# Moving the early ada_w loads to GpSimd's queue and setting the compression's tail one step apart

## The chip, the core and the metric

The kernel runs on one core of one Trainium2 chip. The core has five engines that work beside each other, each in the order of its own queue: TensorE (PE; its weight loads are PEld), VectorE (DVE), ScalarE (ACT), GpSimd (POOL) and SyncE (SP), which here only asks for transfers. A transfer is asked for by an engine's queue and carried out by 16 DMA engines. The metric is the device time of one execution in microseconds, the median of several runs.

## What is computed

One block of a network in float32: 512 tokens of width 2048. Six vectors of 2048 come from one condition row `c`; the first norm, a mixer of convolutions and attention, a residual, the second norm and a gated feed-forward follow. Cut to what the change touches:

```python
sh_a, sc_a, g_a, sh_f, sc_f, g_f = jnp.split(jax.nn.silu(c) @ ada_w[l] + ada_b[l], 6, axis=-1)
h = modulate(rms_norm(x, norm_mix[l]), sh_a, sc_a)
proj = h @ w_in[l]
...
def compress(kv, pe, w1, b1, w2):
    ...
    blocks = kv[:, idx] + pe[None, None, :, None, :]
    hid = jax.nn.gelu(jnp.einsum('bnlgd,ldh->bngh', blocks, w1) + b1)
    return jnp.einsum('bngh,he->bnge', hid, w2)
...
k_cmp = compress(k_cmp_raw, pe_k, k_w1, k_b1, k_w2)
v_cmp = compress(v_cmp_raw, pe_v, v_w1, v_b1, v_w2)
k_cmp = apply_rope(rms_norm(k_cmp, k_norm[0]), cos[:, cmp_end], sin[:, cmp_end])
...
x = x + g_a[:, None, :] * (jnp.concatenate([y_conv, y_attn], axis=-1) @ w_out[l])
h = modulate(rms_norm(x, norm_ffn[l]), sh_f, sc_f)
x = x + g_f[:, None, :] * ((jax.nn.silu(h @ ffn_w1[l]) * (h @ ffn_w3[l])) @ ffn_w2[l])
```

`sh_f`, `sc_f` and `g_f`, which the second half needs, depend on `c` and `ada_w` alone, so they can be summed at any time before.

## The kernel before

Every large product is made of three products of parts: a weight tile is loaded (`raw`), rounded by ScalarE to a high part (`whi`, L92) and completed by VectorE with a low part (`wlo`, L93), and `mm3` (L96 to L100) multiplies the parts. Weight tiles pass through a ring of four `raw`, three `whi` and three `wlo` buffers. PSUM has four banks called `main` for long sums and four called `aux` for everything else.

The stretch around the change is the one between the first stage and the convolutions. Three pieces of work share it:

- `token_blocks` (L702): two blocks of columns of `w_in`, each over 16 chunks of the width, two chunks at a time, for four groups of 128 tokens. That makes 2 x 8 product steps of 24 products; after each the generator yields. The four sums of a block stand in the four `main` banks. `take_kv` and `take_q` read them (`normed_rope`, L514 to L532) and so free the banks, which the convolutions (`conv`, L895) need next.
- `before_attention` (L674): eight norm steps, then `compress` (L576). The compression multiplies blocks of `raw_kv` with its own weights in eight steps (L633), adds the bias into `hid` (L641), takes the Gelu (L642), and ends with a tail: transposes of `hid` (L648) copied to `hidT` (L650), the product `pk` (L653) with norm and rotation (`normed_rope`, which ends in `u` at L531), the transpose of `u` (L657), and the value products (L668) copied to `v4` (L671). Its small late weights and biases are already asked for by GpSimd (L622, L626).
- `early` (L715): the first three of the parts of `ada_w` that the second norm needs, `ffn_part` for j = 0, 1, 2. Each part is summed by `ada` (L173): 16 tiles of 128 x 512 are loaded one by one into a ring of two buffers (`wring`, L512) and added with a factor by VectorE (L187, L189); then four transposes and a reduction (`ada_cols`) write columns of `gsc` or `shf`.

`beside` (L440) lets the early parts take 3, later 2, at last 4.8 of their steps after each product step; `weave` (L102) lets `before_attention` take 1.5 steps after each. A step is the code from one `yield` to the next. This sets the order of the program text. The order in which each queue issues is set from it by a planner, which lets an instruction pass another that it expects to be late; each engine then works through its queue strictly in that order and waits on semaphores.

In the tail there are three yields between the Gelu and the transposes of `hid`, none between these and `pk`, one ahead of the transpose of `u`, and one at the end.

A second, later user of the same functions is `gates_beside` (L959): it sums further parts beside the convolutions, with the tiles of other tensors as places.

## Time and profile before

| | us |
|---|---|
| median of three runs | 2181.52 |
| lowest and highest | 2179.64, 2182.79 |
| span of the profiled execution (first to last instruction) | 2174.9 |
| granted TensorE clock, share of full speed | 0.998 |

The profile is of one execution. Its span is 6.6 us less than the median of the runs; what lies between is ahead of the first and behind the last instruction. A row of a timeline reads: start, length, engine, line, operation, what is written and read, and in brackets how long the engine idled just ahead and what ended that. A row of a waits view reads: who waited, for whom, microseconds in total, times, longest. A landing is the time from the issue of a transfer until its data are there. Product rows have a modelled length and overlap; two starts in a row tell the pace.

### The profile page before, as it was taken

The numbers are of one execution on the slowest core, as the hardware profiler recorded it, in microseconds if no ns is written. First come the engines' busy times: TensorE is split into PE (matmuls) and PEld (weight loads), VectorE is DVE, ScalarE is ACT, GpSimd is POOL, SyncE is SP. The second block draws the span as 40 slices with busy tenths as digits, with TensorE's granted clock in tenths as the row PEclk, the third lists the DMA queues.
The fourth block names the chain that finished last, engine by engine and source line by source line (L and its number), as shares of the span: only waits on it lengthen the run. The fifth ranks groups of instructions, "written<-read, shape, count | busy, mean of one in ns | idle before, by whom it ended". The sixth has DMA issues, their size and how long they took to land.

```text
span 2174.9 us, 31018 instructions
## 1 busy us (share of the span) xinstructions
PE 2143.3 (99%) x11513; PEld 1799.9 (83%) x11513; DVE 1722.8 (79%) x2574; ACT 1007.8 (46%) x1622; POOL 222.9 (10%) x273
## 2 busy tenths in 40 slices
PE   7999999999999999999999999999999999999999
PEld 5788768888888888888888888888888888888887
DVE  5978869977886665988787878888787887878788
ACT  5335334555555223744444444444444455444543
POOL 2410000000000100000000000000000112111210
PEclk9999999999999999999999999999999999999999
DMA  9965768754654985387777777677776499797976
GB/s 339 365 233 166 255 205 256 234 157 148 177 156 138 287 290 170 93 219 185 187 174 175 166 179 185 173 170 171 184 177 172 105 305 284 154 299 143 288 158 142
DMA packets 442315, 438.39 MB, mean 202 GB/s; under 512 B 18468, under 2 KB 349260, under 8 KB 441524
## 3 DMA queue, kind: packets, MB, share of 16 engines
q1 hardware_dynamic: 373184, 327.50, 48.1%
q0 software_dynamic: 68448, 108.44, 24.1%
q8 instruction: 90, 1.47, 0.3%
q14 instruction: 61, 0.50, 0.1%
q10 hardware_dynamic: 532, 0.48, 0.1%
HBM read 416.39 MB, written 19.96 MB: 201 GB/s over the span
## 4 chain that ended last, share of the span: by engine, by line
PE 89%; DVE 5%; DMA 4%; issue 1%; ACT 0%; SPq 0%; DVEq 0%; ACTq 0%
PE main L1209 15%; PE aux L1209 11%; PE aux L1567 9%; PE main L1567 9%; PE main L1211 8%; PE main L98 7%; PE main L99 7%; PE main L100 7%; PE aux L1211 6%; DMA araw<-in_ada_w 2%; PE aux L98 2%; PE aux L100 2%; PE aux L99 2%; DVE acc L189 2%; PE aux L860 1%
## 5 line engine op out<-in xcount | busy, mean ns | idle before, releaser
L1195 ACT CAST whi<-raw 128x1024 fp32r<-128x1024 f32 x246 | 258.0, 1049 | 285.6 <-PE main L1209 107.1
L1209 PE MATMUL main<-hC,whi 128*128 128x512 f32 x1408 | 353.5, 392 | 1.4 <-ACT whi L1195 1.4
L1195 ACT CAST whi<-t 128x1024 fp32r<-128x1024 f32 x186 | 195.4, 1051 | 263.7 <-PE aux L1209 70.3
L1202 DVE TENSOR_TENSOR wlo<-raw,whi 128x1024 fp32r<-128x1024 f32 x218 | 266.1, 1221 | 54.9 <-ACT whi L1195 49.9
L1209 PEld LDWEIGHTS main<-hC,whi 128*128 128x128 f32 x1408 | 253.3, 189 | 47.6 <-ACT whi L1195 1.6
L1209 PE MATMUL aux<-hC,whi 128*128 128x512 f32 x1072 | 268.9, 392 | 0.0
L1209 PEld LDWEIGHTS aux<-hC,whi 128*128 128x128 f32 x1072 | 192.9, 189 | 34.4
L1211 PEld LDWEIGHTS main<-hC,wlo 128*128 128x128 f32 x1408 | 192.0, 190 | 13.6
L1211 PE MATMUL main<-hC,wlo 128*128 128x256 f32 x1408 | 196.3, 282 | 0.0
L98 PE MATMUL main<-alo,whi 128*128 128x512 f32 x448 | 182.3, 407 | 3.6 <-DVE alo L372 2.7
L100 PE MATMUL main<-ahi,whi 128*128 128x512 f32 x448 | 176.4, 394 | 0.0
L99 PE MATMUL main<-ahi,wlo 128*128 128x512 f32 x448 | 176.3, 394 | 0.0
L92 ACT CAST whi<-raw 128x1024 fp32r<-128x1024 f32 (+2 forms) x84 | 79.6, 951 | 203.1 <-PE main L100 124.0
L1211 PEld LDWEIGHTS aux<-hC,wlo 128*128 128x128 f32 x1072 | 146.3, 190 | 10.4
L1211 PE MATMUL aux<-hC,wlo 128*128 128x256 f32 x1072 | 149.6, 282 | 0.0
L1539 DVE TENSOR_TENSOR wlo<-t,whi 128x1024 fp32r<-128x1024 f32 x102 | 124.2, 1220 | 29.1 <-ACT whi L1195 29.0
L1185 POOL DMA_DIRECT2D t<-in_ffn_w x42 | 65.0, 1547 | 794.8 <-DVE d L1216 656.3
L93 DVE TENSOR_TENSOR wlo<-raw,whi 128x1024 fp32r<-128x1024 f32 (+2 forms) x84 | 91.5, 1093 | 51.4 <-ACT whi L92 51.0
L1202 DVE TENSOR_TENSOR wlo<-t,whi 128x1024 fp32r<-128x1024 f32 x84 | 102.6, 1222 | 37.0 <-ACT whi L1195 37.0
L1216 DVE TENSOR_TENSOR d<-aux,d 128x256 f32<-128x256 f32 x168 | 70.9, 422 | 62.2 <-PE aux L1211 62.1
L1567 PE MATMUL aux<-whi,glo 128*128 128x512 f32 x308 | 119.8, 389 | 0.0
L1567 PE MATMUL aux<-whi,ghi 128*128 128x512 f32 x308 | 119.8, 389 | 0.0
(363 smaller groups left out, 4314.0 us busy)
## 6 DMA issues: line engine op xcount, KB each, us to landing
raw<-in_ffn_w SPq DMA_DIRECT2D x204, 512.0 KB, 5.1
t<-in_ffn_w POOLq DMA_DIRECT2D x90, 512.0 KB, 7.5
t<-in_ffn_w SPq DMA_DIRECT2D x78, 512.0 KB, 4.5
araw<-in_ada_w POOLq DMA_DIRECT2D x56, 512.0 KB, 14.4
kT<-in_ada_w SPq DMA_DIRECT2D x100, 256.0 KB, 3.9
raw<-in_w_in SPq DMA_DIRECT2D x128, 192.0 KB, 2.7
araw<-in_ada_w SPq DMA_DIRECT2D x40, 512.0 KB, 7.2
raw<-in_w_in SPq DMA_DIRECT2D x37, 512.0 KB, 9.3
```

The source lines that it names most:

```text
L92: nc.scalar.copy(hi[:, :m], raw[:, :m])
L93: nc.vector.tensor_sub(lo[:, :m], raw[:, :m], hi[:, :m].bitcast(F32))
L98: nc.tensor.matmul(ps, lhs[0], rhs[1], start=first, stop=False)
L99: nc.tensor.matmul(ps, lhs[1], rhs[0], start=False, stop=False)
L100: nc.tensor.matmul(ps, lhs[0], rhs[0], start=False, stop=last)
L1195: hi_ins[-1] = nc.scalar.copy(hi, t).ins
L1202: lo_ins[-1] = nc.vector.tensor_sub(lo, t, hi.bitcast(F32)).ins
L1209: nc.tensor.matmul(ps, wt[0][:, ks[k]], hc(p, k), start=first and k == 0, stop=False, skip_group_check=True)
L1211: nc.tensor.matmul(ps[:, HS:], wt[1][:, ks[k]], hc(p, k)[:, 0:HS], start=False, stop=last and k == HK - 1, skip_group_check=True)
L1216: nc.vector.tensor_add(to, ps[:, h * HS:(h + 1) * HS], to)
L1539: W["last"] = nc.vector.tensor_sub(lo, t, hi.bitcast(F32)).ins
L1567: nc.tensor.matmul(ps[2 * t + c], x_[:, j, tok], w[:, cs], start=m == 0 and j == 0 and p in (1, 5, 2), stop=m == 2 and j == GS[b] - 1 and ...
```

## The change

`ada`, `ffn_part` and `ffn_parts` get an argument `q`, the queue that asks for the `ada_w` tiles; it is SP's where nothing is said, and GpSimd's for `early`. The later users keep SP. In the compression's tail one yield moves from ahead of the transposes of `hid` to behind them, ahead of `pk`, and a second yield is added ahead of the transpose of `u`.

```diff
-    def ada(ring, width, c0, n, got, bias=False):
+    def ada(ring, width, c0, n, got, bias=False, q=nc.sync):
...
-            nc.sync.dma_start(rv, ada_v[:, k0:k0 + step, c0:c0 + n])
+            q.dma_start(rv, ada_v[:, k0:k0 + step, c0:c0 + n])
...
-    def ffn_part(ring_, width, j):
+    def ffn_part(ring_, width, j, q=nc.sync):
...
-            yield from ada(ring_, width, (3 + m) * D + j * 512, 512, got)
+            yield from ada(ring_, width, (3 + m) * D + j * 512, 512, got, q=q)
...
-            yield from ada(ring_, width, 5 * D + cs.start, 512, got, bias=True)
+            yield from ada(ring_, width, 5 * D + cs.start, 512, got, bias=True, q=q)
...
-    def ffn_parts(ring_, width, js):
+    def ffn_parts(ring_, width, js, q=nc.sync):
         for j in js:
-            yield from ffn_part(ring_, width, j)
+            yield from ffn_part(ring_, width, j, q)
...
         yield
         yield
-        yield
         for h in range(2):
             pt = aux()
             nc.tensor.transpose(pt[:, :P], hid[:, h * P:(h + 1) * P], ident)
             for m in range(2):
                 nc.vector.tensor_copy(hidT[:, m, h, :], pt[:, at_m[m]])
+        yield
         pk = aux()
         for h in range(2):
             nc.tensor.matmul(pk[:NP_, :HD], hidT[:, 0, h, :], cw2[0][h], start=h == 0, stop=h == 1)
         u = normed_rope(pk[:NP_, None, :HD], 1, "c", 0, NP_)
+        yield
         yield
         pt = aux()
...
-    early = ffn_parts(wring, 512, range(3))
+    early = ffn_parts(wring, 512, range(3), nc.gpsimd)
```

## The prediction

> **What bounds the kernel now.** First the head of the page.

> ```profile
> span 2174.9 us, 31018 instructions
> ...
> PE 2143.3 (99%) x11513; PEld 1799.9 (83%) x11513; DVE 1722.8 (79%) x2574; ACT 1007.8 (46%) x1622; POOL 222.9 (10%) x273
> ```

> TensorE is busy for 2143.3 of 2174.9 us, so an edit that removes none of its products can give back only waits of TensorE. The edits lie between the end of the first stage and the start of the convolutions, so the second view is who TensorE waited for between 187 and 330 us (total, times, longest).

> ```profile
> PE aux L657 <- DVE ru L531: 1.5, 1, 1.5
> PE aux L653 <- DVE hidT L650: 1.3, 1, 1.3
> PE main L98 <- DVE rq L522: 0.9, 1, 0.9
> PE main L98 <- DVE wlo L93: 0.8, 1, 0.8
> PE main L98 <- DVE rw L529: 0.8, 1, 0.8
> ```

> Five waits, 5.3 us together: this is the whole prize, 0.24% of the time. The first two, 2.8 us, are in the compression's tail. The window from 310 to 320 (PE, PEld, DVE, ACT and POOL busy, granted clock, DMA share, GB/s) has the end of the tail and the last of them.

> ```profile
> 310.00:320.00 10.00, 8.88 (x41) 6.98 (x42) 9.33 (x26) 5.87 (x25) 0.00 (x0) 1.00 0.66 185
> ```

> The clock is full, so nothing is throttled; TensorE has 1.1 us to spare, VectorE only 0.7. What stands behind the waits is told by the chain of waits from 282 to 322 us (start, length, what).

> ```profile
> 314.63 0.76 DVE acc L189
> 315.41 2.78 DMA araw<-in_ada_w
> 318.28 0.75 DVE acc L189
> 319.04 0.33 DVE rw L529
> ...
> 319.52 0.47 PE main L98
> ```

> The reader is to see a ring of two `araw` tiles: a sum (L189) ends, the next load is asked for 0.02 us later (314.63 + 0.76 = 315.39, issue at 315.41), and 2.8 us pass until the tile is there. TensorE's 319.52 product, the first of the convolutions, stands at the end of that ring. The sums' own view from 284 to 320 us gives their count, their length and what VectorE idled for ahead of them (us, times):

> ```profile
> L189 DVE SCALAR_TENSOR_TENSOR acc<-araw,cT,acc x16: 737/752/753, 284.2 to 318.3; 128x512 f32<-128x512 f32 x16
> ...
>   DMA araw<-in_ada_w: 8.7, 7
> ```

> Sixteen sums in 34.1 us are 2.1 us each, 4.3 for a round trip of the two tiles. So VectorE, which works in order, is held up by loads for the second norm, which comes after the attention, and TensorE sees it only where something that it needs stands behind.

> **The tail's steps.** TensorE's timeline, then VectorE's, around the tail, and the Gelu's row of ScalarE:

> ```profile
> 301.98 0.38 PE L648 MATMUL aux<-const,hid 128*128 128x128 f32 x2
> ...
> 302.43 0.40 PE L99 MATMUL main<-whi,alo 128*128 128x512 f32 x1
> 304.10 0.69 PE L653 MATMUL aux<-late,hidT 128*62 128x128 f32 x4 [1.28 <-DVE hidT L650]
> ...
> 308.05 0.39 PE L99 MATMUL main<-whi,alo 128*128 128x512 f32 x1
> 308.27 0.39 PE L100 MATMUL main<-whi,ahi 128*128 128x512 f32 x1
> 310.20 0.24 PE L657 MATMUL aux<-const,ru 62*128 62x62 f32 x1 [1.54 <-DVE ru L531]
> ```

> ```profile
> 293.06 0.87 DVE L641 TENSOR_TENSOR hid<-aux,late 62x256 f32<-62x256 f32 x2
> ...
> 298.48 1.54 DVE L189 SCALAR_TENSOR_TENSOR acc<-araw,cT,acc 128x512 f32<-128x512 f32 x2 [2.98 <-DMA araw<-in_ada_w]
> ...
> 303.83 0.60 DVE L650 COPY hidT<-aux 128x62 f32<-128x62 f32 x4
> ...
> 306.85 0.75 DVE L189 SCALAR_TENSOR_TENSOR acc<-araw,cT,acc 128x512 f32<-128x512 f32 x1 [2.16 <-DMA araw<-in_ada_w]
> ...
> 309.77 0.28 DVE L531 TENSOR_TENSOR ru<-ru,rq 62x128 f32<-62x128 f32 x1
> ...
> 313.41 1.19 DVE L671 COPY v<-aux 32x128 f32<-32x128 f32 x4
> ```

> ```profile
> 295.30 0.42 ACT L642 ACTIVATE hid<-hid 128x256 f32<-128x256 f32 x1
> ```

> A product step is 24 products of the kind of L99 and L100, 0.22 us apart (308.05 to 308.27): 5.3 us. The diff moves the two transposes of `hid` one step earlier and the transpose of `u` one step later, and keeps the product `pk` (L653). It adds no instruction. The moved last step also issues a memset on POOL (L661), which ran 70 us ahead of its use and stays free.

> Transposes of `hid`: they go from 302.0 to about 296.5. The Gelu ends at 295.72, so they can run. Their copies (L650, 0.60) fall into VectorE's idle 2.98 us ahead of 298.48, or right behind that pair of sums, at 300.6; both are ahead of 302.0. The wait of 1.28 goes: **-1.28**.

> Transpose of `u`: `pk` ends at 304.79, `u` (L531) at 310.05, 5.3 us later. One product step is 5.3 us, so with the same delays the wait of 1.54 just closes. Two sums stand in that stretch on VectorE, and each may come later from the other queue (below). I keep 0.5 of the wait: **-1.0**. The ends are -1.54 and 0.

> What follows in that step, the `v` products (L668) and copies, is behind L657 as before and reaches VectorE at nearly the same hour, since the waits ahead of it shrink as it moves back. Cost taken: 0. If it came a whole step later, its copies, twice the 1.19 us of L671, would stand with the first take of the convolutions' main banks, and the wait there would be up to 2.4 longer.

> **The queue.** Forty-eight triggers (three parts of 16 tiles) leave SP for POOL. On SP each takes 0.33 us and nobody waits for SP's time itself, so removing them alone gives 0. The raw tiles of `w_in` behind them would be asked for sooner, and the one wait on their split (0.8, L93) may shrink; no row tells whether its load was late by SP or by the ring's place. Between 0 and -0.8 I take 0.

> On POOL the descriptor work and the landing of loads of the same size (128 rows of 512 floats) show as follows; the first pair of rows is today's load on SP (187 to 330 us), then `k<-gd`, then `cc<-rsd`, each with its landing row (min, median, max), and last the `araw` loads of the first stage, twice as large.

> ```profile
> L183 SPq DMA_DIRECT2D araw<-in_ada_w x46: 327/334/545, 193.5 to 315.4; - x46
> DMA to landing us min/median/max: 2.8/3.7/6.9
> ```
> ```profile
> L1373 POOL DMA_DIRECT2D k<-gd x44: 539/547/595, 1728.6 to 2032.9; - x44
> DMA to landing us min/median/max: 3.0/7.5/12.8
> ```
> ```profile
> L935 POOL DMA_DIRECT2D cc<-rsd x8: 568/574/590, 370.9 to 704.0; - x8
> DMA to landing us min/median/max: 3.4/5.0/5.5
> ```
> ```profile
> L276 POOL DMA_DIRECT2D araw<-in_ada_w x56: 751/751/923, 28.0 to 124.0; - x56
> ```

> The `k` loads come in bursts, so their median holds their own queue; their least, 3.0, is a load alone, 0.2 over SP's least. `cc` reads one row for all partitions; its median is 1.3 over SP's. The trigger is slower as well:

> ```profile
> 106.49 1.54 DVE L291 SCALAR_TENSOR_TENSOR acc<-araw,cT,acc 128x512 f32<-128x512 f32 x2
> ```
> ```profile
> 108.36 0.75 POOL L276 DMA_DIRECT2D araw<-in_ada_w  x1 [1.19 <-DVE acc L291]
> ```

> The sums end at 108.03, POOL starts at 108.36: 0.33 against SP's 0.02. So one round trip of the ring costs 0.51 more (0.31 + 0.2) to 1.61 more (0.31 + 1.3). Below nothing: on SP an `araw` load lines up behind the raw tiles of `w_in`, and its longest landing is 6.9; with a queue of its own the least of 3.0 could come back, so a single round trip may also gain some 3.5. Of the two the lower is nearer, because `k` has the same shape and plain source, and the gain on crowded ones offsets part of it.

> From 293 (where VectorE turns to `hid`, L641) to the first convolution product at 319.5 are 26.5 us, six round trips of 4.3. If VectorE kept its order, that product would come 6 x 0.51 = 3.1 to 6 x 1.61 = 9.7 later. But the order is not the text's: L99 stands between L648 and L653, where the text has no step, so a planner sets it from expected readiness, and a slower ring puts fewer sums ahead of the take. In the last ten microseconds VectorE hardly idles at all (9.33 busy), so there its own work, sums among it, is the limit. Between 0 and the 3.1 to 9.7 I take **0** for the ring, its cover being VectorE's idle 8.7 us and the fact that nobody waits for the sums themselves.

> POOL has other work behind the new triggers:

> ```profile
> 239.19 0.31 POOL L661 MEMSET hrep<- 128x256 f32 x1 [94.51 <-PE aux L584]
> 274.81 0.57 POOL L622 DMA_DIRECT2D late<-in_cmp_k_b  x1 [35.31 <-DVE acc L189]
> ...
> 290.62 0.31 POOL L639 MEMSET hid<- 128x256 f32 x1 [12.56 <-PE aux L633]
> ```

> The memset of `hid` may stand behind a trigger that waits for a sum; VectorE adds at 293.06, over 2 us later, and triggers come some 2.1 us apart, like the sums, so 0, with 2 at the worst. Triggers may stand behind L622, which waited 35.31 us for its buffer; six loads of 0.57 are 3.4 us of POOL once, ahead of the 293 from which I count. I take 0.

> **The sum.** -1.28 - 1.0 + 0 = -2.3 us: span 2174.9 - 2.3 = 2172.6. The median of the runs, 2181.5, lies 6.6 over the profiled span (launch and end); with the same 6.6 the forecast is **2179.2**. A measurement here can tell about 0.2% (4.4 us) from no change, so this counts as no change.

> **Rivals.**
> 1. All goes: with fewer sums ahead of the take, the convolutions' start (0.9) and the split (0.8) go too: 1.28 + 1.54 + 0.9 + 0.8 = 4.5, 2177.0. For it: VectorE's 9.33 just there is partly sums. Against: it needs every wait to close. Chance 0.18.
> 2. A wait takes the place of those removed: the chain shows the ring, not the tail, ahead of 319.52. TensorE gets there 2.3 earlier and waits 2.3 longer for L529; or the planner puts the tail's pieces where they stood. 2181.5. Chance 0.18.
> 3. Slower: the ring at POOL's price with sums still ahead of L529. Place: VectorE's queue ahead of the first `q` take. It decides from the point where six round trips cost more than the tail gives back at the convolutions, and is beyond 4.4 from 0.73 a trip on. 3.1 to 9.7 dearer, 2184.6 to 2191.2, about 2187. For it: the median of `cc`. Against: planned order, and loads no longer behind raw tiles. Chance 0.22.

> [...]

> **How the numbers follow.** Forecast 0.42, rivals 0.18, 0.18 and 0.22. Faster by over 0.2% (under 2177.2): most of rival 1 and the forecast's edge, 0.18. Slower (over 2185.9): most of rival 3 and a little of 2, 0.20. Within: 0.62. The range goes from rival 1 with a margin, 2176.0, to the middle of rival 3, 2187.0.

> **What would show it.** Right: L653 and L657 gone from TensorE's waits, `hidT` copied a product step ahead of `pk`, loads from POOL landing in 3 to 4 us, first convolution product near 317. Wrong: that product at or after 319.5 behind sums that wait for `araw`; landings of 5 us and more; POOL's memset of `hid` after 293; or a shift past 330 us, where nothing was edited.

## The result, and the profile after

The kernel became slower: 2192.12 us against 2181.13 us (medians of five runs each, 2190.40 to 2195.49 and 2179.35 to 2182.79), a ratio of 1.0055 with a 95% interval from 1.0043 to 1.0067. That is 12 us by the ratio, or 11.0 by the medians. The prediction's range ended at 2187.0.

The head of the page after (span, and the busy line of section 1):

```profile
span 2190.3 us, 31035 instructions
PE 2151.1 (98%) x11513; PEld 1806.8 (82%) x11513; DVE 1722.9 (79%) x2574; ACT 1007.1 (46%) x1622; POOL 248.3 (11%) x321
```

TensorE runs the same 11513 products and is busy 7.8 us longer with them. POOL has 48 instructions more, the triggers, and 25.4 us more of busy time.

The two spans differ by 15.4 us, more than the medians, because the profiled execution before was a quick one (its span lies 6.6 us under the median, that of after 1.8) and because the stretch starts at another time in each. So the stretch itself is measured. (In every run listed the time lies 1.7 to 2.1 us over its span. So of the 6.6 us that the part on the time before, and the prediction's sum after it, put ahead of the first and behind the last instruction, some 4.8 are only that quick execution.) These are TensorE's timelines before and after, at the first product of the token blocks and at the first of their ninth step:

```profile
200.57 0.50 PE L98 MATMUL main<-wlo,ahi 128*128 128x512 f32 x1
...
255.16 0.48 PE L98 MATMUL main<-wlo,ahi 128*128 128x512 f32 x1
```

```profile
203.22 0.50 PE L98 MATMUL main<-wlo,ahi 128*128 128x512 f32 x1
...
264.75 0.78 PE L98 MATMUL main<-wlo,ahi 128*128 128x512 f32 x1
...
335.54 0.39 PE L98 MATMUL main<-alo,whi 128*128 128x512 f32 x1
```

The last row is the first product of the convolutions, which stood at 319.52 before. From the first token product to it passed 319.52 - 200.57 = 118.95 us, and now 335.54 - 203.22 = 132.32 us. The **stage** is 13.4 us longer; from its end to the end of the kernel pass 1855.4 us before and 1854.8 us after. So nothing is lost or won behind it. All runs below are read by this length of the stage, beside their times.

Who TensorE waited for from 187 to 345 us, after (total, times, longest):

```profile
PE main L98 <- DVE wlo L93: 3.5, 2, 2.9
PE aux L540 <- DVE ru L531: 2.4, 1, 2.4
PE aux L553 <- DVE ru L531: 2.2, 1, 2.2
PE aux L658 <- DVE ru L531: 2.2, 1, 2.2
PE aux L669 <- DVE hrep L665: 1.4, 1, 1.4
```

That is 11.7 us where it was 5.3. The wait for `hidT` is gone, as forecast, but the one for `u` (L657, now L658) grew, and waits of 2.2 to 2.9 us have come far ahead of the tail. The second half of the loss is in the granted clock (windows of the page after; the last three columns are the clock, the DMA share and GB/s):

```profile
230.00:240.00 10.00, 10.00 (x42) 8.10 (x40) 8.14 (x19) 4.22 (x13) 1.61 (x3) 0.83 0.61 180
260.00:270.00 10.00, 7.78 (x40) 5.64 (x37) 9.48 (x29) 1.32 (x6) 1.30 (x3) 0.83 0.85 281
290.00:300.00 10.00, 7.06 (x32) 4.87 (x31) 4.43 (x5) 2.09 (x2) 4.04 (x8) 0.83 0.69 217
320.00:330.00 10.00, 6.44 (x26) 4.56 (x24) 6.76 (x20) 2.60 (x10) 1.07 (x2) 0.80 0.52 156
330.00:340.00 10.00, 10.00 (x43) 8.09 (x43) 8.37 (x20) 6.01 (x28) 0.00 (x0) 0.86 0.15 39
```

The slow stretches run at half rate (0.50 in a window cut to one, in the last section), so a clock of 0.83 over 10 us is 3.4 us of it (2 x 0.17 x 10); the last two rows together are 4.0 + 2.8. So TensorE ran some 17 us at half rate, which costs up to 8.5 us; before, the clock was full through the stage (1.00 in every window of 10 us). One place shows how the two hang together. VectorE's, POOL's and TensorE's timelines after, near 294 us:

```profile
293.51 0.75 DVE L189 SCALAR_TENSOR_TENSOR acc<-araw,cT,acc 128x512 f32<-128x512 f32 x1 [4.67 <-DMA araw<-in_ada_w]
294.18 2.35 DVE L93 TENSOR_TENSOR wlo<-raw,whi 128x1024 fp32r<-128x1024 f32 x2
```

```profile
291.87 0.55 POOL L183 DMA_DIRECT2D araw<-in_ada_w  x1
294.56 0.54 POOL L183 DMA_DIRECT2D araw<-in_ada_w  x1 [2.14 <-DMA araw<-in_ada_w]
```

```profile
295.46 0.79 PE L98 MATMUL main<-wlo,ahi 128*128 128x512 f32 x1 [2.94 <-DVE wlo L93]
296.05 0.63 PE L99 MATMUL main<-whi,alo 128*128 128x512 f32 x1
296.48 0.63 PE L100 MATMUL main<-whi,ahi 128*128 128x512 f32 x1
```

VectorE idles 4.67 us for a tile of `ada_w` that nobody needs yet; the split of a weight tile that TensorE does need stands behind that sum, though its high part was ready at 291.32 (ScalarE's row, 290.27 + 1.05). TensorE waits 2.94 us for it, and its next products start 0.43 us apart (296.05 to 296.48) where 0.22 is its pace at full clock. The sum ends at 294.26 and the next load starts on POOL at 294.56, 0.30 later; on SP that was 0.02.

What VectorE waited for from 187 to 345 us, before and then after:

```profile
DVE acc L189 <- DMA araw<-in_ada_w: 19.0, 14, 3.7
```

```profile
DVE acc L189 <- DMA araw<-in_ada_w: 31.9, 25, 4.7
```

So 14 waits for a tile became 25, and 12.9 us more: about the length by which the stage grew. That is no proof by itself, since part of the growth is the clock. The ring after, in the chain of waits of the same kind as before:

```profile
308.20 0.77 DVE acc L189
308.97 0.29 issue
309.25 2.91 DMA araw<-in_ada_w
312.25 0.76 DVE acc L189
313.01 0.28 issue
313.30 3.03 DMA araw<-in_ada_w
```

A link that was not there before, 0.28 us from the sum's end to the trigger, now stands in each trip. The loads' rows after, with their landing (min, median, max):

```profile
L183 POOL DMA_DIRECT2D araw<-in_ada_w x46: 537/537/547, 196.4 to 323.6; - x46
DMA to landing us min/median/max: 2.9/3.3/6.4
```

The row of before, 2.8/3.7/6.9, holds only the five of its 46 loads whose landing the trace tells, so the two rows can't be set side by side closely. They show a later trigger and no later landing; the comparison at a held order, below, is closer.

### The profile page after: what moved, and what is told of

Same layout as the page of the kernel before. It is cut to its first block, busy times and chain, and to the rows that moved or that the text cites. A ratio compares the mean times of both kernels' runs of the same rounds, so it can differ in the third digit from the quotient of the medians.

```text
span 2190.3 us, 31035 instructions
## 1 busy us (share of the span) xinstructions
PE 2151.1 (98%) x11513; PEld 1806.8 (82%) x11513; DVE 1722.9 (79%) x2574; ACT 1007.1 (46%) x1622; POOL 248.3 (11%) x321
## 4 chain that ended last, share of the span: by engine, by line
PE 89%; DMA 5%; DVE 4%; issue 2%; ACT 0%; POOL 0%; DVEq 0%; SPq 0%; POOLq 0%; ACTq 0%
PE main L1210 15%; PE aux L1210 11%; PE aux L1568 9%; PE main L1568 9%; PE main L1212 8%; PE main L98 7%; PE main L100 7%; PE main L99 7%; PE aux L1212 6%; DMA araw<-in_ada_w 3%; PE aux L98 2%; PE aux L100 2%; PE aux L99 2%; PE aux L861 2%; PE aux L852 1%
## 5 line engine op out<-in xcount | busy, mean ns | idle before, releaser
L1203 DVE TENSOR_TENSOR wlo<-raw,whi 128x1024 fp32r<-128x1024 f32 x218 | 265.7, 1219 | 54.6 <-ACT whi L1196 52.4
L1212 PEld LDWEIGHTS main<-hC,wlo 128*128 128x128 f32 x1408 | 192.0, 190 | 13.6
L98 PE MATMUL main<-alo,whi 128*128 128x512 f32 x448 | 181.9, 406 | 2.7 <-DVE alo L372 2.7
L100 PE MATMUL main<-ahi,whi 128*128 128x512 f32 x448 | 176.2, 394 | 0.0
L99 PE MATMUL main<-ahi,wlo 128*128 128x512 f32 x448 | 175.7, 392 | 0.0
L93 DVE TENSOR_TENSOR wlo<-raw,whi 128x1024 fp32r<-128x1024 f32 (+2 forms) x84 | 91.4, 1092 | 51.2 <-ACT whi L92 50.6
L189 DVE SCALAR_TENSOR_TENSOR acc<-araw,cT,acc 128x512 f32<-128x512 f32 x109 | 81.7, 749 | 53.3 <-DMA araw<-in_ada_w 51.7
```

The lines of the kernel that those rows point to most:

```text
L93: nc.vector.tensor_sub(lo[:, :m], raw[:, :m], hi[:, :m].bitcast(F32))
L98: nc.tensor.matmul(ps, lhs[0], rhs[1], start=first, stop=False)
L99: nc.tensor.matmul(ps, lhs[1], rhs[0], start=False, stop=False)
L100: nc.tensor.matmul(ps, lhs[0], rhs[0], start=False, stop=last)
L189: nc.vector.scalar_tensor_tensor(acc, w, s, acc, op0=ALU.mult, op1=ALU.add)
L1203: lo_ins[-1] = nc.vector.tensor_sub(lo, t, hi.bitcast(F32)).ins
```

## The experiments

Three questions: which part of the change costs, is it the ring of two tiles, and is it the queue itself or the order in which the planner sets the work for it. "Order" is counted from VectorE's timeline: how many of the 48 early sums stand ahead of each of the last eight of the sixteen splits (`wlo`, L93) of the token weights.

| kernel | sums ahead of splits 9 to 16 |
|---|---|
| before | 24, 26, 29, 31, 32, 34, 35, 39 |
| after | 24, 26, 31, 34, 34, 36, 38, 42 |

### One part of the change at a time

First the tail alone, then the queue alone:

```diff
-    early = ffn_parts(wring, 512, range(3), nc.gpsimd)
+    early = ffn_parts(wring, 512, range(3))
```

> The tail's steps as changed, the ada_w tiles asked for by SP as before. Theory A (the loss is the two-tile ring, whose round trip is dearer from GpSimd's queue: about 0.27 us later trigger and 0.3 us later landing, some 24 trips): nothing of the loss is here; the time is 0 to 3 us under before, 2178 to 2181, VectorE waits some 19 us for araw and TensorE shows no half clock in the stage. Theory B (the tail's steps, set apart, bring the last products and the reading of the banks too late): most of the 11 us is here, 2187 to 2192.

> The tiles asked for by GpSimd as changed, the tail's steps as before. Theory A: the whole loss, 2190 to 2195, VectorE's waits for araw near 32 us, the clock halved some times in the stage. Theory B: near before, 2180 to 2184.

The tail alone took 2182.05 us (ratio 1.0006, 0.9997 to 1.0016), the queue alone 2192.69 us (1.0056, 1.0040 to 1.0073). The loss is the queue's, all of it: the second run lies in theory A's range. The first is 1 us above theory A's, and its VectorE order is that of before, while the queue alone has the order of after. The tail's gain did not come either; TensorE's waits with the tail alone show why:

```profile
PE aux L658 <- DVE ru L531: 2.2, 1, 2.2
PE main L98 <- DVE rw L529: 0.9, 1, 0.9
```

The wait for `hidT` (1.3) is gone, and the one for `u` is 2.2 where it was 1.5. One stretch of 3.4 us at half clock, which theory A did not expect, stands behind it.

### Four tiles, wider tiles, and the late loads

The ring of four lies in the second half of `q`, which is not written yet then:

```diff
+    class Four:
+        n = 0
+
+        def tile(self, shape, dtype, tag, name):
+            self.n += 1
+            return qT[1][:, self.n % 4, :]
+
-    early = ffn_parts(wring, 512, range(3), nc.gpsimd)
+    early = ffn_parts(Four(), 512, range(3), nc.gpsimd)
```

> The changed kernel with a ring of four tiles (the unwritten half of qT) in place of two. Theory A: a load has twice the time to come, so VectorE's waits for araw fall from 32 us to under 10, the half clock goes, and the time is at or under before, 2174 to 2181. Theory C (GpSimd's queue itself is the trouble: triggers stand behind the six late loads, the memsets and other triggers that wait): the waits stay at the place of the late loads, at 288 to 295 us, and the time stays over before, 2184 to 2190.

> The tail's steps as changed, SP's queue, a ring of four tiles. Theory A: VectorE's waits for araw fall from 19 us to under 8 as well, and as the waits of TensorE in this stretch (5.3 us before) stand behind them, the time falls to 2175 to 2179. If the ring alone explains nothing of before's waits, it is equal to the run with the tail alone.

By POOL's queue 2188.06 us (1.0032, 1.0021 to 1.0043), by SP's 2179.24 us (0.9996, 0.9987 to 1.0006). Four tiles give back some 5 us of the 12, and SP's queue with the same ring is still about 8 us quicker. So theory A's 2174 to 2181 was missed by POOL's queue, and theory C's range met; VectorE still waits 13.0 us for tiles there. But the order moved too: 28, 29, 36, 44, 44, 48, 48 and 48 sums ahead of the last eight splits by POOL's queue, 29, 33, 36, 39, 40, 43, 44 and 48 by SP's.

Next the six late loads (L622, L626) by SP's queue, with the ring of two and with the ring of four, and a ring of two tiles twice as wide, with one load for two sums:

```diff
-                    nc.gpsimd.dma_start(late[0][at_m[m], :256], a[b1n].to_broadcast([NP_, 256]))
+                    nc.sync.dma_start(late[0][at_m[m], :256], a[b1n].to_broadcast([NP_, 256]))
...
-                        nc.gpsimd.dma_start(cw2[m][h], a[w2n][0, h * P:(h + 1) * P, :])
+                        nc.sync.dma_start(cw2[m][h], a[w2n][0, h * P:(h + 1) * P, :])
```

> The changed kernel with one difference: the six late loads of the compression's tail (L622 and L626) go to SyncE's queue, so that GpSimd's queue holds the sums' loads and three memsets alone. Theory (two-tile ring's round trip): each of about 24 round trips of the stage is some 0.5 us dearer by GpSimd and the late loads touch only one of them, so 2190 to 2192 us, with VectorE's waits for araw still near 30 us. Rival (GpSimd's queue is blocked: the late loads hold GpSimd from 288.7 to 291.9 us and delay one sum's load by 3.2 us, behind which the weight splits of 295 us stand): 2187 to 2189 us, the half clock at 295 us gone.

> The ring of four tiles by GpSimd's queue (2188.06 us before), with the six late loads on SyncE's queue. There the profile shows loads asked for at 285.9 and 286.7 us landing 7.3 and 7.6 us later, among them the late loads, and a weight split waiting 3.0 us at 295 us behind those sums. Rival of the blocked queue: 3 us come back, about 2185 us. Theory that the sums' loads run beside the weights' loads and delay them, whatever is behind them on GpSimd: 2187 to 2189 us.

> The changed kernel with the sums' ring made of two tiles of 128x1024 in the second half of q, not yet written then: one load of 512 KB serves two sums, so half as many round trips by GpSimd's queue with the same bytes. Theory (what counts is the number of round trips times their added length): half of the 11 us that the queue costs come back, so about 2186.5 us (2185 to 2188.5), like the ring of four. Rival (the loss is that loads by a second queue run beside the weights' and take their bandwidth): larger loads in flight make it no better, 2190 to 2194 us. Rival (the loss is GpSimd's time for issuing, 0.54 us each): halved too, so this run does not part it from the theory.

With the ring of two, 2193.01 us (1.0049, 1.0034 to 1.0064): nothing comes back, so the late loads are not seen to cost there, as far as a run tells whose order moved as well (31, 35, 37, 38, 40 and 44 ahead of splits 11 to 16). With the ring of four, 2184.52 us (1.0015, 1.0005 to 1.0024), 3.5 us less than without, as the rival of the blocked queue had said. The wide tiles gave 2192.59 us (1.0048, 1.0032 to 1.0065), a miss for the theory, inside the range of the rival by bandwidth: half as many trips, no gain. VectorE's and TensorE's waits with the wide tiles:

```profile
DVE acc L189 <- DMA qT<-in_ada_w: 10.3, 8, 2.9
```

```profile
PE main L98 <- DVE wlo L93: 7.9, 5, 4.4
```

VectorE waited only 10.3 us for these tiles, but the order had moved: 40, 43, 48, 48, 48, 48, 48 and 48 sums now stood ahead of the last eight splits, and TensorE waited 7.9 us for splits. So trips alone don't explain the time, and this run can't tell bandwidth from order; the order had to be held.

### Two half loads by SP's queue

Each tile asked for by two loads of 64 partitions, with the old tail:

```diff
-            nc.sync.dma_start(rv, ada_v[:, k0:k0 + step, c0:c0 + n])
+            for h in range(parts):
+                hp = slice(h * P // parts, (h + 1) * P // parts)
+                nc.sync.dma_start(rv[hp], ada_v[hp, k0:k0 + step, c0:c0 + n])
```

> The kernel before, on SyncE's queue with the two-tile ring, but each sum's tile is asked for by two loads of 64 partitions, one behind the other: the last half is issued 0.34 to 0.4 us later, bytes unchanged. Theory (round trip of the two-tile ring, some 24 of them with VectorE waiting): 24 x 0.36 = 8.6 us, so 2188 to 2191 us without GpSimd having any part in it, VectorE's wait for araw rising from 19 to 27 us or more and half clocks appearing in the stage. Rival (the loss is GpSimd's own: its issuing, its descriptors, its order): 2181 to 2184 us.

2178.99 us (0.9990, 0.9980 to 0.9999), below the theory's range and the rival's: the expectation of the round trip fell, as long as the planner may set the order anew. It set 21, 23, 25, 27, 28, 30, 32 and 33 sums ahead of the last eight splits, fewer than before.

### Sums held among the splits

An edge of order (`NoSync` in the diff) sets one instruction behind another on its engine. Here each split is held behind the sums that stand ahead of it in the other kernel, and the next sum behind the split:

```diff
+    def behind(late, first):
+        tc.add_manual_dep(late, first.name, mybir.DependencyInfo(
+            mybir.DependencyClass.NoSync, mybir.DependencyReason.DATA), reason="order")
+
+    own = sums[first_sum:]
+    for low, n in zip(splits[first_split:], (2, 3, 5, 7, 11, 13, 15, 17, 24, 26, 29, 31, 32, 34, 35, 39)):
+        behind(low, own[n - 1])
+        if n < len(own):
+            behind(own[n], low)
```

> The changed kernel with its sums bound, by edges of order alone, to the places that they have in the kernel before among the sixteen token weight splits of VectorE: ahead of them 2, 3, 5, 7, 11, 13, 15, 17, 24, 26, 29, 31, 32, 34, 35 and 39 sums, where the changed kernel has 16 and 18 ahead of the seventh and eighth and 31, 34, 34, 36, 38 and 42 ahead of the last six. Queue, ring, tiles and the tail stay those of the changed kernel. Theory (order: the planner takes a load that no longer stands in SyncE's queue for an earlier one and sets more sums, each a round trip of 3.7 us, ahead of the splits): most of the 11 us come back, 2182 to 2186 us. Rival (round trip by GpSimd's queue is longer by itself): the same sums still stand ahead of the first twelve splits, 2188 to 2192 us.

> The mirror of it: the kernel before, with SyncE's queue and the old tail, whose sums are bound to the places that they have in the changed kernel (16 and 18 ahead of the seventh and eighth split, 31, 34, 34, 36, 38 and 42 ahead of the last six, the compression's sum of hid behind 38). Theory (order): 2 to 3 more round trips of 3.15 us ahead of the splits of 280 us and later, 2186 to 2190 us. Rival (GpSimd's round trip): 2181 to 2183 us.

> The ring of four by GpSimd's queue with the late loads on SyncE's (2184.52 us), its sums bound to the places that they have with the same ring on SyncE's queue (29, 33, 36, 39, 40, 43, 44 and 48 ahead of the last eight splits, where it had 28, 29, 36, 44, 48, 48, 48 and 48). Theory (order): 2179.5 to 2182 us, the weight split of 290 us no longer behind eight sums in a row. Rival (what is left is the queue's round trip or its overtaking of the weights' loads): 2183.5 to 2185.5 us.

> The ring of four on SyncE's queue with the new tail (2179.24 us), its sums bound to the places that they have by GpSimd's queue (28, 29, 36, 44, 47, 48, 48 and 48 ahead of the last eight splits). Theory (order): 2182.5 to 2186 us, with a wait of TensorE for the split at 290 us or so. Rival (GpSimd's queue itself): 2179 to 2181 us.

Ring of two: 2189.35 us by POOL with the order of before (1.0032, 1.0022 to 1.0042), 2183.19 us by SP with the order of after (1.0007, 0.9998 to 1.0017). The first lies in its rival's range: some 5 us of the 12 come back. The second is 0.2 above its rival's, and not told apart from nothing. Ring of four: 2183.79 us by POOL with SP's order (1.0009, 1.0000 to 1.0019), 2187.20 us by SP with POOL's order (1.0024, 1.0015 to 1.0034). The first of these lies in its rival's range; the last, 1.2 above its theory's, is the clearest: the queue, the ring and the tail of the 2179.24 us kernel, other places for its sums, and 8 us more. The wait that appeared there on TensorE:

```profile
PE main L100 <- DVE wlo L95: 10.4, 3, 8.5
```

(L95 is the split, two lines lower in that kernel.) But these edges hold only sums and splits and, where POOL's order is set on SP's queue, the compression's sum of `hid`; the other steps of VectorE were still set freely.

### Every step held

So every instruction of VectorE (223), TensorE (540) and ScalarE (112) from the first sum to the start of the convolutions was bound to the order of the other kernel, both ways, with the old tail:

```diff
+    for line in ORDER:
+        names = line.split()
+        for x, y in zip(names, names[1:]):
+            tc.add_manual_dep(log["I-" + y], "I-" + x, mybir.DependencyInfo(
+                mybir.DependencyClass.NoSync, mybir.DependencyReason.DATA), reason="order")
```

(`ORDER` lists the instructions of each engine in the order wanted; `log` finds them. The calls of the three engines go through one helper there, so the profile shows their line as L77.)

> The queue moved alone (old tail, ring of two, loads by GpSimd's queue, 2192.69 us), with every instruction of VectorE (223), TensorE (540) and ScalarE (112) between the first sum and the start of the convolution bound to the order that it has in the kernel before. Theory (order): 2181 to 2184 us, no half clock. Rival (round trip of GpSimd's queue by itself): 2187 to 2192 us, VectorE's wait for araw near 30 us, waits of TensorE over 2 us with half clocks behind them.

> The mirror: the kernel before, loads by SyncE's queue, with every instruction of the three engines in that stretch bound to the order that the planner makes when the loads go by GpSimd's queue. Theory (order): 2188 to 2193 us, with half clocks. Rival (round trip): 2181 to 2184 us.

The traces bear the edges out: in the stage the rows of VectorE, TensorE and ScalarE come in the same sequence as in before for the first run, and as in the queue moved alone for the mirror. SP's other loads were not bound; one or two of the compression's changed places.

| ring of two, old tail | order made for SP's queue | order made for POOL's queue |
|---|---|---|
| loads by SP's queue | 1 (before, 2181.08 us) | 1.0028, 1.0018 to 1.0039 (2187.28 us) |
| loads by POOL's queue | 1.0039, 1.0025 to 1.0054 (2190.23 us) | 1.0056, 1.0040 to 1.0073 (2192.69 us) |

Each alone costs, the queue 8.5 us by its ratio and the order 6.1, and together 12.2: they add up within their intervals. So the first run has its rival's time and the second, but for 0.7 us, its theory's: both have a part. With POOL's queue and the order of before, VectorE's waits and TensorE's are:

```profile
DVE acc L77 <- DMA araw<-in_ada_w: 27.2, 22, 4.8
```

```profile
PE aux L77 <- DVE ru L77: 4.0, 4, 1.4
PE main L77 <- DVE wlo L77: 2.7, 2, 1.5
PE aux L77 <- DVE hidT L77: 2.1, 1, 2.1
PE main L77 <- DVE rq L77: 1.8, 1, 1.8
PE main L77 <- DVE rw L77: 1.2, 1, 1.2
```

27.2 us in 22 waits, 8.2 more than the 19.0 of before at the very same order: 0.37 us for each waited trip. The loads of this run, from the view of the tile `araw`:

```profile
L206 POOL DMA_DIRECT2D araw<-in_ada_w x46: 537/537/548, 197.6 to 326.5; - x46
...
DMA to landing us min/median/max: 2.7/3.5/6.6
```

The median time from a sum's end to the trigger is 0.30 us, where it was 0.03 by SP's queue. Since the trace tells so few landings of SP's, take the 14 sums for whose tile VectorE waited in both runs: from the trigger's start to the sum's start they took 0.10 us longer by the median (0.08 by the mean, single ones from 2.1 less to 2.7 more), and from the releasing sum's end 0.38. So most of the price is the later trigger, 22 x 0.27 = 5.9 of the 8.2 us; what the rest is isn't told apart.

Two other ways in which the queue could cost are not seen. One trigger came 3.2 us late, behind the six late loads, but VectorE waited 1.2 us for its tile, and 1.3 in before. Nor did the weights come later, as the rival by bandwidth has it: VectorE waited 4.4 us for ScalarE's high parts, and 5.4 in before.

TensorE's waits are 11.8 us, none over 2.1, and the clock stayed full (1.00 in every window of 10 us): the stage is 126.38 us, 7.4 longer. That execution was the quickest of the five, 2188.26 us at a granted clock of 0.998; two others had 0.995, which by an estimate is 13 us more at half clock (2 x 0.003 x 2190), though no trace shows where.

The mirror, SP's queue with POOL's order, has TensorE's waits at 11.6 us, two of them long, and these windows:

```profile
260.00:270.00 10.00, 7.15 (x22) 5.53 (x23) 8.34 (x28) 2.55 (x8) 0.00 (x0) 0.66 0.96 325
290.00:300.00 10.00, 6.36 (x31) 4.38 (x30) 5.67 (x7) 2.09 (x2) 0.00 (x0) 0.83 0.69 229
300.00:310.00 10.00, 10.00 (x45) 7.26 (x45) 5.49 (x8) 2.92 (x3) 0.31 (x1) 0.83 0.90 293
```

Some 13.6 us at half rate with not one load by POOL's queue among the early ones. So the half clock isn't the queue's doing; it comes where TensorE waits.

### The half loads again, with the order held

The same half loads by SP's queue as above, and quarter loads, with every step bound to the order of before:

> SyncE's queue, each sum's tile asked for by two loads of 64 partitions, and all three engines bound to the order of before, so that the round trip is longer by one more issue (0.34 to 0.4 us) and nothing else changes. Theory (what counts is the length of the round trip at a given order): 2183 to 2188 us. Rival (length does not count, or two half loads land sooner than one whole): 2178 to 2182 us.

> The same with four loads of 32 partitions, three more issues, about 1.1 us more for each round trip. Theory (length of the round trip): 2190 to 2200 us, and half clocks in the stage. Rival: 2178 to 2184 us.

2201.44 us (1.0091, 1.0074 to 1.0107) and 2227.58 us (1.0213, 1.0197 to 1.0228), both far over the theory's ranges. VectorE's wait for tiles with half loads, first with the planner's own order, then with that of before:

```profile
DVE acc L191 <- DMA araw<-in_ada_w: 15.7, 6, 6.6
```

```profile
DVE acc L77 <- DMA araw<-in_ada_w: 42.1, 21, 9.7
```

The loads, the queue and the ring are the same; the order alone makes 2178.99 or 2201.44 us of them. The dose is not a clean one: the 46 added loads also lengthen SP's line, and the load behind the wait of 9.7 us was asked for at 292.84 us, beside two loads of `w_in` and POOL's six late loads, five of which took 7.2 to 8.2 us to land. It shows that a late tile is paid for at a given order, not how much a tenth of a microsecond costs.

### A version that is quicker than both

> The kernel before with one change: the early sums' tiles are four of 128x512 in the second half of q, loads by SyncE's queue. Theory (round trip and order): VectorE's waits for the tiles fall from 19 to some 11 us, the stage from 119 to 117 us, so 2178.5 to 2180.5 us. Rival (the ring was never what ended the waits): 2180.5 to 2182 us.

> The ring of four on SyncE's queue with the new tail (2179.24 us), its sums bound to later places among the weight splits: 2, 3, 5, 6, 9, 11, 14, 16, 21, 23, 25, 27, 28, 30, 32 and 33 ahead of the sixteen, as the planner set them for the two half loads (2178.99 us), where it set 3, 3, 6, 8, 12, 15, 16, 18, 29, 33, 36, 39, 40, 43, 44 and 48. Theory (each sum ahead of a split can hold it): the waits of TensorE for the splits, 2.4 us there, go; 2176.5 to 2179 us. Rival (the sums only move their cost to after the last split): 2179 to 2183 us.

The ring of four by SP's queue with the old tail took 2180.28 us beside 2182.40 for before on the same chip (0.9985, 0.9976 to 0.9994); with the new tail and the sums held to the later places of the half loads' order, 2178.32 us (0.9982, 0.9974 to 0.9991), some 4 us less than before and 16 less than after by their ratios. Both times lie in their theories' ranges. In the last one VectorE waits 2.4 us for tiles instead of 19.0, and TensorE's waits are

```profile
PE main L100 <- DVE rw L532: 2.8, 2, 2.3
PE aux L672 <- DVE hrep L668: 1.2, 1, 1.2
PE aux L661 <- DVE ru L534: 0.5, 1, 0.5
```

4.5 us: the waits for splits are gone, as expected, but others came, and the ring of four alone had 3.1. What the later places add to the ring of four isn't told apart from nothing by these intervals.

### The account of the stage

| kernel | stage, us | TensorE's waits in it | at half clock | 118.95 + (waits - 5.3) + half clock / 2 |
|---|---|---|---|---|
| before | 118.95 | 5.3 | 0 | 118.95 |
| after | 132.32 | 11.7 | 17.0 | 133.9 |
| POOL's queue, order of before | 126.38 | 11.8 | 0 | 125.5 |
| SP's queue, POOL's order | 130.60 | 11.6 | 13.6 | 132.1 |
| ring of four, SP, new tail | 117.19 | 3.1 | 0 | 116.8 |
| ring of four, POOL, new tail | 125.01 | 7.4 | 10.2 | 126.2 |

The last column is worked out from the two before it. It meets the stage within 2 us in these rows, and in every other run with no wait over 5 us. With the ring of four by SP's queue in POOL's order it is 4 us too high (126.47 us of stage, 11.6 of waits, 10.2 at half clock), since part of the slow stretch lay inside the wait of 8.5 us; with the half loads and the quarter loads at the order of before, whose longest waits are 8.7 and 14.3 us, it is 4 and 13 too high. This is an account of where TensorE's time went; what made its waits is told by the runs above.

## Why the prediction was wrong

**What bounds the kernel** was right: TensorE in its work, and in the stage a ring of two tiles through VectorE. That the prize was 5.3 us is not contradicted, since no kernel here came more than 4 us under the one before; that the waits could also grow was priced too low.

**The tail's steps, -2.3 forecast.** Wrong by its size. The wait for `hidT` closed; the wait for `u` did not shrink by 1.0 but grew by 0.7 with the tail alone (1.5 to 2.2), and a stretch at half clock came with it. Measured: +1.1 us by the medians, not told apart from nothing. That is what the second rival had said, for the tail alone.

**The queue, 0 forecast: the step that failed.** It was "Between 0 and the 3.1 to 9.7 I take **0** for the ring, its cover being VectorE's idle 8.7 us". Measured: 1.0056, 12 us. Three things stood in its place.
- The price of one trip was about right (0.51 at least was taken; 0.37 was measured at a held order), though of its two parts the trigger's was 0.27 and the landing's 0.1, and though the landing was priced against a row of SP's that holds five loads. But the prediction counted it over six trips from 293 us on. VectorE waits for a tile 14 times in the whole stage before, and 22 to 25 times with POOL's queue: 8.2 us more at the held order, where the stage is 7.4 longer. Half of the loss stands ahead of 293: the ninth product step starts at 264.75, 61.5 us into the stage, where it was 255.16 - 200.57 = 54.6 before, 6.9 us of the 13.4.
- VectorE's idle time was named as cover. It is none: it is the wait itself, and what TensorE needs stands behind it in VectorE's order. The first product of the convolutions, which the prediction set near 317, came at 335.54.
- "A slower ring puts fewer sums ahead of the take" was wrong in sign. The planner set more of them ahead of the splits (31, 34, 34, 36, 38, 42 for 29, 31, 32, 34, 35, 39), and all 48 ahead of the last take, where it had set 46. Why it does so is not shown; that it costs is, 1.0028 on SP's own queue.

**POOL's other work, 0 forecast**, was not contradicted for the ring of two: moving the late loads away gave nothing. The memset of `hid` did come after 293, at 306.13, as the prediction's list of signs against it had it, but neither VectorE nor TensorE waited for it in the profile after.

**The third rival** had the sign and the mechanism, 3.1 to 9.7 dearer with a chance of 0.22, and the range was cut at its middle. Even its upper end, 2191.2, is 0.9 below the median; what lay beyond it are the trips ahead of 293 us, the order, and the clock, which the prediction left at "full, so nothing is throttled". With the 14 trips on which the profile before already shows VectorE waiting, 14 x 0.51 = 7.1 us, this rival would have been the forecast; that they would become 25 could not be read there.

One load and one trigger, beside the prediction's least price of a trip (0.2 for the landing, 0.31 for the trigger): in the 14 sums compared above, the tile came 0.10 us later by the median when counted from the trigger's start, and 0.38 when counted from the sum that releases it; the first is within the spread of single loads. The 46 triggers after took 537 to 547 ns each, no more than the prediction's row of `k` loads (539 to 595).

## What to carry to other kernels

Count a ring's round trip over every trip on which its consumer waits, from the first to the last, not over the stretch beside the edit, and don't take the idle time of an in-order engine for cover: it may be the very wait that holds up what the bounding engine needs. Work that nobody needs yet belongs in a ring deep enough that the in-order engine waits less for it (0.9985 here, with VectorE's wait for tiles at 11.1 us beside 19.0), or behind what TensorE needs, which on top of the deeper ring wasn't told apart from nothing; moving its loads to another queue does neither. When an edit lets a planner set the order anew, hold the order and move the resource, then hold the resource and move the order: here each cost half as much as both together, or more.

## What the runs showed of the hardware that was not expected

**Half clock behind short waits.** In the kernel before, no wait of TensorE in the stage is over 1.5 us and the clock is full; with POOL's queue at the order of before, none is over 2.1 and it is full; after, four waits of 2.2 to 2.9 us come with four stretches at half clock, of 3.4, 3.4, 3.4 and 6.8 us. One run, the ring of four by POOL's queue in SP's order, had a wait of 2.6 us without one.

```profile
261.12:264.53 3.41, 1.19 (x11) 0.48 (x8) 3.41 (x12) 1.07 (x6) 0.54 (x1) 1.00 0.70 177
264.53:267.94 3.41, 3.41 (x10) 2.74 (x11) 3.41 (x13) 0.25 (x1) 0.00 (x0) 0.50 1.01 360
```

```profile
255.61:259.02 3.41, 1.86 (x16) 0.90 (x12) 3.39 (x10) 2.03 (x10) 1.08 (x2) 1.00 0.89 273
259.02:262.43 3.41, 1.54 (x8) 1.32 (x9) 3.41 (x9) 0.29 (x1) 0.00 (x0) 1.00 0.95 335
```

In the first, TensorE was busy for 1.19 of 3.41 us, so it idled for 2.2, and the next step ran at half clock. In the second the wait falls on two steps, with 1.6 and 1.9 us idle, and the clock stays full. Over the 20 traces of this case, in the stage and the 5 us behind it, every step at full clock with more than 1.87 us idle (33 of them) was followed by one at half clock, and none with less than 1.85. No run moved a wait along the grid on purpose, so this is a regularity of these traces and not an experiment. By it a wait of 2 to 3 us is a matter of where it falls; when it counts, a stretch of 3.4 us at half clock costs up to 1.7 us more than the wait shows.

**A trigger by POOL's queue** starts 0.28 to 0.30 us after the sum that releases it has ended, and one by SP's 0.02 to 0.03. From the trigger's start on, the tiles took about as long (0.10 us more by the median of 14 trips, within their spread).
